# Moving the tiles of the weights' low parts to a pool that begins 128 bytes behind a whole row

## The chip, the cores and the metric

The kernel runs on 1 core of one Trainium2 chip. The metric is the device time of one execution in microseconds (us): the median of three timed runs. One further execution was recorded by the hardware profiler, and the rows below come from it.

## The reference

Two model blocks run one after the other on `x` of shape (1, 512, 1024), in float32. The first block has two layers. Each layer is a gated feed-forward network, a mixer with three branches (a Fourier mix, a dilated window attention, a differential attention) and another gated feed-forward network:

```
x = x + 0.5 * swiglu(rmsnorm(x, g_ffn1[l]), w_ffn1_gate[l], w_ffn1_up[l], w_ffn1_down[l])
u = rmsnorm(x, g_mix[l]);  p = u @ w_in[l]
merged = gates[0] * (fourier(p) @ w_br_a) + gates[1] * (dilated(p) @ w_br_b) + gates[2] * (diff(p) @ w_br_c)
x = x + merged @ w_out[l]
x = x + 0.5 * swiglu(rmsnorm(x, g_ffn2[l]), w_ffn2_gate[l], w_ffn2_up[l], w_ffn2_down[l])
```

The second block has one layer of stick-breaking attention beside a state-space mixer, and one layer of gated linear attention. Most of the arithmetic is products of the 512 tokens with weight matrices.

## The kernel before

**Products in three matmuls.** A float32 product is made from operands that are cut in two: `hi`, the value rounded to the type that TensorE takes at one column per cycle (float32r), and `lo`, what is left. `mm3` (L195 to L199) issues hi x hi (L197), hi x lo (L198) and lo x hi (L199) into the same bank of PSUM. `split` (L90 to L95) makes the two parts: ScalarE (ACT) copies the source into `hi` (L93), VectorE (DVE) subtracts `hi` from the source into `lo` (L94).

**Weights.** A chunk of weights is a block of up to 8 x 256 columns on 128 partitions. `weights` (L97) issues one DMA on SP's queue into a raw tile `wr`, then writes `wh` on ACT (L108) and `wl` on DVE (L109), in two halves of 128 columns. `weights7` (L113) does the same for a product that is made from seven smaller ones: `wh` and `wl` hold the parts of four of its operands, and tiles `sw` those of the other three. `setup` (L269) makes the first chunk, `odd` (L1496) one of 128 columns.

**How a chunk is used.** In `form_a`, `form_a2`, `form_a_late` and `form_a7` the weights are the stationary operand (loaded by a LDWEIGHTS, row PEld in the profile) and the tokens `xh`, `xl`, `g` or `sb` are the moving operand, 512 or 256 columns. In `form_b` it is the other way round: the tokens are loaded, and 256 columns of `wh` or `wl` move. In the profile a matmul's name is `b<-moving,stationary`, so `b<-xh,wl` at L199 loads a block of `wl` and moves `xh`.

**Order and waits.** The program is written in one order for each engine. The Tile framework puts in the waits, by the bytes that instructions read and write. TensorE (PE) works through the list; DMA, ACT and DVE prepare the next chunks while it does, two buffers for each of `wr`, `wh` and `wl`.

**Where the tiles lie.** Pools of tiles lie one behind the other in a partition of SBUF. A tile of 512 float32 takes 2,048 bytes; this is the row that the title speaks of. The pool `cp` has the eight tiles `x`, which begin 128 bytes behind a whole row, and constants: the identity `cc` begins 928 bytes behind a whole row (416 behind a multiple of 512), `ntri` 960 and `nones` 448 (both 448 behind a multiple of 512). The pool `wp` begins on byte 36,864, which is 18 whole rows, with `wr`, `wh` and `wl`, two buffers of 8,192 bytes each. The pool `sp` follows, with tiles of 2,048 bytes (`g`, `sw`, `s`, `xh`, `xl`) and four of 5,120 (`sb`). A block that TensorE loads is 128 columns, 512 bytes. So each of L197 to L199's operands begins at a multiple of 512 bytes. The pool `sm`, with tiny tiles of sums and scales, is last.

Of the kernel before, what the change touches and what calls it, by code (L numbers as in the profile page):

```python
# [9 lines left out]
F32 = mybir.dt.float32  # L10
F32R = mybir.dt.float32r
# [6 lines left out]
P = 128  # L18
S = 512
D = 1024  # L20
KD = D // P
# [29 lines left out]
class Kern:  # L51
    def __init__(self, ctx, tc, ins, out, dbg=None):
        self.tc, self.nc, self.ins, self.out, self.dbg = tc, tc.nc, ins, out, dbg
        self.cp = ctx.enter_context(tc.tile_pool(name="cp", bufs=1))
        self.wp = ctx.enter_context(tc.tile_pool(name="wp", bufs=2))
        self.sp = ctx.enter_context(tc.tile_pool(name="sp", bufs=2))
        self.sm = ctx.enter_context(tc.tile_pool(name="sm", bufs=8))
        self.ps = ctx.enter_context(tc.tile_pool(name="ps", bufs=8, space=PSUM))
        self.dp = ctx.enter_context(tc.tile_pool(name="dp", bufs=1, space=DRAM))
        self.n = 0  # L60

    def nm(self, s):
        self.n += 1
        return f"{s}{self.n}"
# [25 lines left out]
    def split(self, src, hi=None, lo=None):  # L90
# [3 lines left out]
        self.nc.vector.tensor_tensor(out=lo, in0=src, in1=hi.bitcast(F32), op=ALU.subtract)  # L94
        return hi, lo  # L95

    def weights(self, src, k0=0, nk=None):  # L97

        nc = self.nc
        src = src[:, k0:k0 + nk, :] if nk is not None else src  # L100
        _, nk, n = src.shape
        raw = self.wp.tile([P, nk, n], F32, tag="wr", name=self.nm("wr"), bufs=2)
        nc.sync.dma_start(raw, src)
        hi = self.wp.tile([P, nk, n], F32R, tag="wh", name=self.nm("wh"))
        lo = self.wp.tile([P, nk, n], F32R, tag="wl", name=self.nm("wl"))
        for j in range(0, n, P):
            js = slice(j, j + P)
            nc.scalar.activation(hi[:, :, js], raw[:, :, js], AF.Copy)  # L108
            nc.vector.tensor_tensor(out=lo[:, :, js], in0=raw[:, :, js], in1=hi.bitcast(F32)[:, :, js],  # L109
                                    op=ALU.subtract)  # L110
        return hi, lo

    def weights7(self, src):  # L113


        nc = self.nc
        raw = self.wp.tile([P, KD, 256], F32, tag="wr", name=self.nm("wr"), bufs=2)
        nc.sync.dma_start(raw, src)
        hi = self.wp.tile([P, KD, 256], F32R, tag="wh", name=self.nm("wh")).rearrange("p k n -> p (k n)")
        lo = self.wp.tile([P, KD, 256], F32R, tag="wl", name=self.nm("wl")).rearrange("p k n -> p (k n)")  # L120
        h = KD // 2
        v3 = lambda t: t.rearrange("p (k n) -> p k n", n=P)
        a = {(i, j): raw[:, j * h:(j + 1) * h, i * P:(i + 1) * P] for i in range(2) for j in range(2)}
        at = [v3(hi[:, i * S:(i + 1) * S]) for i in range(4)], [v3(lo[:, i * S:(i + 1) * S]) for i in range(4)]

        def parts(x, i=None):
            o = (at[0][i], at[1][i]) if i is not None else (v3(self.spare("sw", 6, F32R)), v3(self.spare("sw", 6, F32R)))
            return self.split(x, *o)

        both = v3(hi[:, 0:2 * S]), v3(lo[:, 0:2 * S])  # L130
        self.split(raw[:, :, 0:P], *both)
        a11, a12 = [(at[0][i], at[1][i]) for i in range(2)]
        a22 = parts(a[1, 1], 2)
        s1, s2 = v3(self.spare("s", 2)), v3(self.spare("s", 2))
        self.tt(s1, a[1, 0], a[1, 1], ALU.add)
        p1 = parts(s1, 3)
        self.tt(s2, s1, a[0, 0], ALU.subtract)
        p2 = parts(s2)
        self.tt(s1, a[0, 0], a[1, 0], ALU.subtract)
        p3 = parts(s1)  # L140
        self.tt(s2, a[0, 1], s2, ALU.subtract)
        p4 = parts(s2)
        return {1: a11, 2: a12, 3: p4, 4: a22, 5: p1, 6: p2, 7: p3}
# [125 lines left out]
    def setup(self):  # L269
        nc, ins = self.nc, self.ins  # L270
        self.x = [self.const([P, S], f"x{k}") for k in range(KD)]
        cols = self.const([P, NPAR], "par")
        nc.sync.dma_start(cols, ins["params"])
        warm = self.const([P, 1], "warm")
        nc.vector.memset(warm, 0.0)
        self.act(warm, warm, AF.Silu)

        raw, hi, lo = (self.wp.tile([P, KD, 256], dt, tag=t, name=self.nm(t), bufs=2)
                       for t, dt in (("wr", F32), ("wh", F32R), ("wl", F32R)))
        for k in range(KD):  # L280
            if k % 2 == 0:
                ks = slice(k, k + 2)
                nc.sync.dma_start(raw[:, ks, :], ins["w_ffn1_gate"][0][0][:, ks, :])
                self.split(raw[:, ks, :], hi[:, ks, :], lo[:, ks, :])
            nc.sync.dma_start(self.x[k], ins["x"][k])
        self.first = hi, lo
        self.par, at = {}, 0
        for name, n in PARAMS:
            self.par[name] = cols[:, at:at + n]
            at += n  # L290
        cc = self.const([P, NCONST], "cc")
        nc.sync.dma_start(cc, ins["c_mats"])
        self.ident, self.tri = cc[:, 0:P], cc[:, P:2 * P]
        self.ones = self.const([P, P], "ones")
        nc.vector.memset(self.ones, 1.0)
        one = self.const([P, 2], "one")
        nc.vector.memset(one[:, 0:1], -0.5)
        nc.vector.memset(one[:, 1:2], E32)
        self.mhalf, self.e32 = one[:, 0:1], one[:, 1:2]
        self.nones, self.ntri = self.const([P, P], "nones"), self.const([P, P], "ntri")  # L300
        nc.vector.memset(self.nones, -1.0)
        self.ts(self.ntri, self.tri, -1.0, ALU.mult)
        self.bglu = self.const([P, 4], "bglu")
        self.ts(self.bglu, self.par["s5_b_glu_2"], 0.5, ALU.mult)
        self.bh = self.const([P, 48], "bh")
        self.ts(self.bh, self.par["b_gate"], 0.5, ALU.mult)
# [1189 lines left out]
    def odd(self):  # L1496
# [5 lines left out]
        raw = self.wp.tile([P, KD, P], F32, tag="wr", name=self.nm("wr"), bufs=2)  # L1502
        gp.memset(raw, 0.0)
        nc.sync.dma_start(raw[:, :, 0:16], ins["odd_w_r"])
        w = (self.wp.tile([P, KD, P], F32R, tag="wh", name=self.nm("wh")),
             self.wp.tile([P, KD, P], F32R, tag="wl", name=self.nm("wl")))
        self.split(raw, *w)
        wgt = self.g()
        gp.memset(wgt, 0.0)
# [336 lines left out]
```

## Time and profile before

| | |
|---|---|
| median of three runs | 3041.65 us (3041.04 to 3041.98) |
| the profiled execution's own time | 3038.39 us |
| its span, first to last instruction | 3036.7 us |
| granted clock of TensorE, mean | 1.0 |
| PE busy | 3015.5 us |
| PEld busy | 2645.0 us |
| DVE busy | 2037.7 us |
| ACT busy | 1352.4 us |
| DMA | 311.14 MB, 102 GB/s mean |

The busy time of PE is the time in which at least one matmul was under way. Matmuls are pipelined: the next begins before the last has ended, so the duration of one is longer than the time that it costs. What a matmul costs in a full stream is the distance from its start to the start of the next, which is read from the timeline.

### The profile page before, as it was taken

To read this page: it belongs to the slowest core of one execution; us is meant where nothing else is said; L and a number is where in the kernel's file an instruction comes from. 1 tells how busy PE (TensorE), PEld (TensorE's weight loads), DVE (VectorE), ACT (ScalarE), POOL (GpSimd) and SP (SyncE) were. 2 spreads that over 40 slices of the span, in tenths; PEclk is the share of its full clock that TensorE was granted. 3 is DMA by queue.
4 is the path that set the end of the run, shared out by engine and by line. 5 is a ranking of instruction groups with operands and counts; after the bars stand their busy time and mean duration, and the time that the engine had idled before them with its cause. 6 is when DMAs were issued, how large, how long until landed. Compare 5 with 4: busy or idle time off the path is not lost.

```text
span 3036.7 us, 44149 instructions
## 1 busy us (share of the span) xinstructions
PE 3015.5 (99%) x17718; PEld 2645.0 (87%) x17718; DVE 2037.7 (67%) x3646; ACT 1352.4 (45%) x2380; POOL 177.8 (6%) x310
## 2 busy tenths in 40 slices
PE   9999999999999999999999999999999999999999
PEld 7898889889889988889988889888999898877887
DVE  7798745646567979878874565557788855554633
ACT  5343435544343435433433554444334456663532
POOL 1001000000000011001120000000000011110010
PEclk9999999999999999999999999999999999999999
DMA  4232333322222333223343432222232332312221
GB/s 153 105 103 105 118 108 115 111 78 98 92 90 98 114 121 121 98 98 110 107 140 108 122 108 91 75 97 91 104 112 89 124 131 100 108 53 84 95 70 56
DMA packets 73358, 311.14 MB, mean 102 GB/s; under 512 B 18836, under 2 KB 20564, under 8 KB 44608
## 3 DMA queue, kind: packets, MB, share of 16 engines
q1 hardware_dynamic: 59680, 282.39, 27.0%
q10 hardware_dynamic: 9296, 16.47, 1.9%
q0 software_dynamic: 4176, 9.46, 1.2%
q8 instruction: 139, 2.28, 0.3%
q14 instruction: 67, 0.55, 0.1%
HBM read 292.47 MB, written 12.66 MB: 100 GB/s over the span
## 4 chain that ended last, share of the span: by engine, by line
PE 94%; ACT 2%; issue 1%; DVE 1%; DMA 1%; POOL 0%; SPq 0%; POOLq 0%; ACTq 0%; DVEq 0%
PE b L197 29%; PE b L199 29%; PE b L198 29%; PE b L202 7%; PE b L266 2%; ACT g L250 1%; ACT L250 0%; ACT sb L250 0%; DMA g<-tb 0%; DVE wl L109 0%; POOL sb L1259 0%; POOL y L240 0%; DVE g L240 0%; DMA g<-s_kst 0%; DMA wr<-in_w_ffn_gate 0%
## 5 line engine op out<-in xcount | busy, mean ns | idle before, releaser
L197 PE MATMUL b<-xh,wh 128*128 128x512 f32 (+1 forms) x1880 | 692.6, 368 | 7.3 <-ACT xh L250 6.8
L198 PE MATMUL b<-xl,wh 128*128 128x512 f32 (+1 forms) x1880 | 682.4, 363 | 1.1 <-DVE xl L94 1.1
L199 PE MATMUL b<-xh,wl 128*128 128x512 f32 (+1 forms) x1880 | 682.8, 363 | 0.5 <-DVE wl L94 0.5
L108 ACT ACTIVATE wh<-wr 128x1024 fp32r<-128x1024 f32 (+2 forms) x396 | 383.2, 1005 | 537.2 <-PE b L198 350.3
L109 DVE TENSOR_TENSOR wl<-wr,wh 128x1024 fp32r<-128x1024 f32 (+2 forms) x396 | 453.2, 1162 | 137.0 <-ACT wh L108 135.4
L197 PE MATMUL b<-g,wh 128*128 128x512 f32 x1168 | 456.6, 391 | 0.5 <-ACT g L93 0.5
L199 PE MATMUL b<-g,wl 128*128 128x512 f32 x1168 | 454.8, 389 | 1.2 <-DVE wl L109 1.2
L198 PE MATMUL b<-g,wh 128*128 128x512 f32 x1168 | 454.8, 389 | 0.2 <-DVE g L94 0.2
L197 PEld LDWEIGHTS b<-xh,wh 128*128 128x128 f32 x1880 | 355.7, 189 | 62.4 <-ACT xh L250 6.8
L198 PEld LDWEIGHTS b<-xl,wh 128*128 128x128 f32 x1880 | 355.8, 189 | 57.3 <-issue 2.2
L199 PEld LDWEIGHTS b<-xh,wl 128*128 128x128 f32 x1880 | 355.2, 189 | 57.8 <-DVE wl L94 0.9
L240 DVE TENSOR_TENSOR g<-b,g 128x512 f32<-128x512 f32 (+2 forms) x265 | 184.2, 699 | 235.3 <-PE b L199 220.8
L199 PEld LDWEIGHTS b<-g,wl 128*128 128x128 f32 x1168 | 219.2, 188 | 47.9 <-DVE wl L109 2.0
L197 PEld LDWEIGHTS b<-g,wh 128*128 128x128 f32 x1168 | 219.3, 188 | 47.5 <-issue 2.0
L198 PEld LDWEIGHTS b<-g,wh 128*128 128x128 f32 x1168 | 219.3, 188 | 45.3 <-DVE g L94 0.5
L197 PE MATMUL b<-wh,xh 128*128 128x256 f32 x896 | 256.9, 287 | 0.0
L198 PE MATMUL b<-wl,xh 128*128 128x256 f32 x896 | 254.5, 284 | 1.0 <-DVE wl L109 1.0
L199 PE MATMUL b<-wh,xl 128*128 128x256 f32 x896 | 253.6, 283 | 0.0
L240 DVE TENSOR_TENSOR g<-g,g 128x512 f32<-128x512 f32 (+8 forms) x371 | 200.8, 570 | 66.7 <-ACT g L250 62.3
L240 DVE TENSOR_TENSOR g<-g,b 128x256 f32<-128x256 f32 (+1 forms) x484 | 176.9, 397 | 31.2 <-PE b L199 27.3
L93 ACT ACTIVATE sw<-s 128x512 fp32r<-128x512 f32 x180 | 111.8, 630 | 193.3 <-DVE s L240 159.2
L250 ACT ACTIVATE g<-g 128x512 f32<-128x512 f32 (+4 forms) x280 | 143.6, 528 | 96.5 <-DVE g L240 88.3
(242 smaller groups left out, 5117.2 us busy)
## 6 DMA issues: line engine op xcount, KB each, us to landing
wr<-in_w_ffn_up SPq DMA_DIRECT2D x44, 1024.0 KB, 4.8
wr<-in_w_ffn_gate SPq DMA_DIRECT2D x43, 1024.0 KB, 4.8
wr<-in_w_ffn_down SPq DMA_DIRECT2D x32, 1024.0 KB, 4.8
wr<-in_w_gate SPq DMA_DIRECT2D x24, 1024.0 KB, 4.8
wr<-in_w_in SPq DMA_DIRECT2D x20, 1024.0 KB, 4.8
wr<-in_even_w_in SPq DMA_DIRECT2D x20, 1024.0 KB, 5.1
wr<-in_w_ffn_down SPq DMA_DIRECT2D x16, 768.0 KB, 4.3
g<-tb ACTq DMA_DIRECT2D x48, 256.0 KB, 3.1
```

The source lines that it names most:

```text
L93: self.nc.scalar.activation(hi, src, AF.Copy)
L108: nc.scalar.activation(hi[:, :, js], raw[:, :, js], AF.Copy)
L109: nc.vector.tensor_tensor(out=lo[:, :, js], in0=raw[:, :, js], in1=hi.bitcast(F32)[:, :, js], op=ALU.subtract)
L197: t.matmul(out, l[0], r[0], start=start, stop=False)
L198: t.matmul(out, l[0], r[1], start=False, stop=False)
L199: t.matmul(out, l[1], r[0], start=False, stop=stop)
L202: self.nc.tensor.matmul(out, l, r, start=start, stop=stop)
L240: return (eng or self.nc.vector).tensor_tensor(out=out, in0=a, in1=b, op=op)
L250: self.nc.scalar.activation(out, a, f, **kw)
L266: self.nc.tensor.transpose(out, a, self.ident)
```

## The change

A new pool `lp` with two buffers of 8,192 bytes takes the tiles `wl`, and a pool `pp` ahead of it has one tile of 128 bytes that nothing uses. Each `wl` is now a view of a flat tile of 2,048 elements; its bytes inside the tile are in the same order as before. `wp` is shorter by 16,384 bytes, so that the tiles of `sp` lie eight rows lower, still on the same place in a row. `sp` ends on byte 204,800, which is 100 whole rows, and the two `wl` begin 128 bytes behind a whole row, at 204,928 and 213,120. No instruction is added or taken away, and the calls are in the same order.

```diff
         self.sp = ctx.enter_context(tc.tile_pool(name="sp", bufs=2))
+        self.pp = ctx.enter_context(tc.tile_pool(name="pp", bufs=1))
+        self.lp = ctx.enter_context(tc.tile_pool(name="lp", bufs=2))
         self.sm = ctx.enter_context(tc.tile_pool(name="sm", bufs=8))
...
+        self.pp.tile([P, 32], F32, name="pad")
...
+    def low(self, nk, n):
+
+        t = self.lp.tile([P, KD * 256], F32R, tag="wl", name=self.nm("wl"))
+        return t[:, 0:nk * n].rearrange("p (k n) -> p k n", n=n)
+
     def weights(self, src, k0=0, nk=None):
...
-        lo = self.wp.tile([P, nk, n], F32R, tag="wl", name=self.nm("wl"))
+        lo = self.low(nk, n)
...
-        lo = self.wp.tile([P, KD, 256], F32R, tag="wl", name=self.nm("wl")).rearrange("p k n -> p (k n)")
+        lo = self.low(KD, 256).rearrange("p k n -> p (k n)")
...
-        raw, hi, lo = (self.wp.tile([P, KD, 256], dt, tag=t, name=self.nm(t), bufs=2)
-                       for t, dt in (("wr", F32), ("wh", F32R), ("wl", F32R)))
+        raw, hi = (self.wp.tile([P, KD, 256], dt, tag=t, name=self.nm(t), bufs=2) for t, dt in (("wr", F32), ("wh", F32R)))
+        lo = self.low(KD, 256)
...
-             self.wp.tile([P, KD, P], F32R, tag="wl", name=self.nm("wl")))
+             self.low(KD, P))
```

## Rows read from the trace of the kernel before

**Rows 1.** The page: busy time of each engine, share of the span, instructions.
```profile
PE 3015.5 (99%) x17718; PEld 2645.0 (87%) x17718; DVE 2037.7 (67%) x3646; ACT 1352.4 (45%) x2380; POOL 177.8 (6%) x310
```

**Rows 2.** Waits of PE: for whom, us in total, times, longest.
```profile
PE b L197 <- ACT xh L250: 6.8, 1, 6.8
...
PE b L199 <- DVE wl L109: 1.2, 1, 1.2
...
PE b L198 <- DVE wl L109: 1.0, 1, 1.0
...
PE b L199 <- DVE wl L94: 0.5, 1, 0.5
```

**Rows 3.** PE's groups by line and shape: count | busy us, mean ns | idle before.
```profile
L199 PE MATMUL b<-xh,wl 128*128 128x512 f32 x1400 | 547.0, 391 | 0.5 <-DVE wl L94 0.5
...
L199 PE MATMUL b<-g,wl 128*128 128x512 f32 x1168 | 454.8, 389 | 1.2 <-DVE wl L109 1.2
...
L198 PE MATMUL b<-wl,xh 128*128 128x256 f32 x896 | 254.5, 284 | 1.0 <-DVE wl L109 1.0
...
L199 PE MATMUL b<-xh,wl 128*128 128x256 f32 x480 | 135.8, 283 | 0.0
...
L199 PE MATMUL b<-sb,wl 128*128 128x256 f32 x480 | 135.8, 283 | 0.0
```

**Rows 4.** PE's timeline, 512 columns, behind other work: start us, duration, instruction.
```profile
442.86 0.39 PE L198 MATMUL b<-xl,wh 128*128 128x512 f32 x1
443.09 0.40 PE L199 MATMUL b<-xh,wl 128*128 128x512 f32 x1
...
445.17 0.39 PE L199 MATMUL b<-xh,wl 128*128 128x512 f32 x1
...
447.66 0.39 PE L198 MATMUL b<-xl,wh 128*128 128x512 f32 x1
```

**Rows 5.** PE's timeline, 256 columns, weights moving.
```profile
476.89 0.28 PE L197 MATMUL b<-wh,xh 128*128 128x256 f32 x1
477.01 0.28 PE L198 MATMUL b<-wl,xh 128*128 128x256 f32 x1
...
478.81 0.28 PE L198 MATMUL b<-wl,xh 128*128 128x256 f32 x1
```

**Rows 6.** Busy time in two stretches: PE, PEld, DVE, ACT, POOL, clock, DMA.
```profile
444.90:452.00 7.10, 7.10 (x44) 6.25 (x44) 1.93 (x8) 2.49 (x7) 0.00 (x0) 1.00 0.54 181
477.00:482.00 5.00, 5.00 (x45) 5.00 (x43) 4.12 (x9) 2.77 (x7) 0.00 (x0) 1.00 0.77 228
```

**Rows 7.** PE's timeline, plain float32 matmuls with constants or tokens loaded.
```profile
2484.41 0.59 PE L202 MATMUL b<-g,nones 128*128 128x256 f32 x2
2484.84 0.59 PE L202 MATMUL b<-sb,ntri 128*128 128x256 f32 x2
2485.27 0.39 PE L202 MATMUL b<-sb,nones 128*128 128x128 f32 x2
2485.49 0.28 PE L202 MATMUL b<-sb,ntri 128*128 128x128 f32 x1
...
2498.09 2.32 PE L202 MATMUL b<-sb,g 128*128 128x512 f32 x8
2500.17 0.36 PE L197 MATMUL b<-wh,xh 128*128 128x256 f32 x1
```

**Rows 8.** Groups of DVE and ACT by line and shape.
```profile
L109 DVE TENSOR_TENSOR wl<-wr,wh 128x1024 fp32r<-128x1024 f32 x328 | 395.1, 1221 | 117.0 <-ACT wh L108 115.4
...
L240 DVE TENSOR_TENSOR g<-g,g 128x512 f32<-128x512 f32 x219 | 145.3, 687 | 64.0 <-ACT g L250 61.5
...
L240 DVE TENSOR_TENSOR x<-x,g 128x512 f32<-128x512 f32 x96 | 65.9, 688 | 1.7
...
L250 ACT ACTIVATE g<-g,y 128x512 f32<-128x512 f32 x80 | 57.1, 715 | 81.1 <-DVE y L244 81.1
...
L250 ACT ACTIVATE xh<-x,par 128x512 fp32r<-128x512 f32 x56 | 39.6, 715 | 55.3 <-DVE x L247 24.4 <-DVE x L240 23.8 <-PE b L199 7.0
```

## The prediction

> **What bounds the kernel now.** I read the page's first part, then PE's waits, then PE's groups by shape, then its timeline. The first shows that PE is the bound: it is busy for 3015.5 us of 3036.7, where DVE has 2037.7 and ACT 1352.4 [rows 1]. The second shows that it hardly ever waits for the tiles that are moved: 1.2, 1.0 and 0.5 us, one wait each [rows 2]. So a low part that is ready sooner, or a DVE that writes it faster, is worth 2.7 us at most, 0.09%. What can move the time is the distance from one matmul's start to the next.
>
> That distance is in the timeline. In a settled stream of 512 columns, 11 matmuls go from 445.17 to 447.66: 226.4 ns each [rows 4]. In a stream of 256 columns, 16 go from 476.89 to 478.81: 120.0 ns each [rows 5]. The granted clock is 1.00 in both stretches [rows 6], the 2.4 GHz level, at which 512 columns are 213.3 ns and 256 are 106.7. So each matmul of `mm3` costs 13 ns more than its columns, whether it has 512 or 256.
>
> Plain float32 matmuls go over their operand twice (two records for each), and there the extra is almost gone: two records of 256 columns go from 2484.84 to 2485.27, 215 ns each, and two of 128 from 2485.27 to 2485.49, 110 ns each [rows 7]. 215 and 110 against 226.4 and 120.0 is what a matmul of `mm3` could at best lose: 11.4 and 10.0 ns.
>
> **The change, part by part.** No instruction is added, removed or reordered, and no transfer. Three things are different: where `wl` lies, where the tiles of `sp` lie, and how `wl` is described to the framework.
>
> *DVE and ACT.* 328 pieces of 1,024 elements at L109 take 1221 ns [rows 8]; they now write at another place of a row. The nearest rows for such a place are the tiles `x`, which begin 128 bytes behind a row already: adding into `x` takes DVE 688 ns, and the same shape among `g`, on whole rows, 687; ACT reads `x` in 715 ns and `g` in 715 [rows 8]. So nothing changes there. If a piece were longer by 10 ns, 328 of them are 3.3 us, beside PE, which waits 2.7 us for them in the whole run [rows 2]; and if that cover were gone the 3.3 us would be the cost. I take 0.
>
> *`sp` eight rows lower.* Each tile keeps its place in a row. I take 0; the settled 226.4 and 120.0 hold over tiles of many rows, so that which rows meet seems to cost nothing.
>
> *TensorE.* A low part is read by PE in two ways. As the stationary operand of L199: 1400 + 1168 = 2568 matmuls of 512 columns and 480 + 480 = 960 of 256. As the moving operand of L198: 896 of 256 [rows 3]. That is 2568 long and 1856 short matmuls. Up to now the two operands that PE reads at a time in `mm3` both begin at a multiple of 512 bytes; in these 4424 they will be 128 bytes apart in that sense. The trace has no matmul of `mm3` with another place, so I bound the cost from both sides by the nearest rows.
>
> Below: all of the extra goes, 2568 x 11.4 ns + 1856 x 10.0 ns = 29.3 + 18.6 = 47.9 us. Above: the stream behaves as it does behind other work. From 443.09 to 445.17 nine matmuls take 231.1 ns each, before it settles at 226.4 [rows 4]; 2568 x 4.7 ns = 12.1 us, or 36.2 us if all three matmuls of each product (7704) stay unsettled. For 256 columns I take no loss.
>
> Which end is near? Three things speak for nothing at all. First, the float32 matmuls with a constant loaded (448 behind a multiple of 512) take 0.86 us for 1,024 columns from 2484.41 to 2485.27, 0.84 ns a column; those with tokens loaded, both operands on a multiple, take 2.08 us for 2 x (512 + 384 + 256 + 128) = 2,560 columns from 2498.09, 0.81 ns [rows 7]. Meeting at the same place is no dearer there. Second, from 477 to 482 DVE was busy for 4.12 us of 5.00, ACT for 2.77 and DMA at 0.77 [rows 6], and the 120.0 ns inside it [rows 5] did not move; if places in SBUF collided, theirs should show too. Third, the extra is the same 13 ns for 512 and 256 columns, though the loads fill 6.25 of 7.10 us of the one stretch and all of the other [rows 6]. That looks like a price of each matmul. Against it stands the unsettled stretch [rows 4]: a fixed price would not be 18 ns in one stretch and 13 in the next, with the same tiles and lines, where only the phase between loading and moving can differ. So the two streams do touch each other, and a shift might matter. I take 0 and keep both ends.
>
> The Trainium skill gives two rules here that pull apart. TensorE: Matmul & The Clock Gate, section Back-to-back issue gap, has N / 2.4 + 2.5 ns for a warm stream, 215.8 ns for 512 columns; the 226.4 of the trace is longer, so by that page 10.6 ns of each long matmul are something that could go, 27 us over the 2568. SBUF — State Buffer, section Who interferes with whom, gives PE two independent read ports and says that PE never waits on anyone; by it the place of a tile costs nothing and the sum is 0. The trace agrees with neither entirely: the gap is longer than the first has it, and the unsettled stretch is not what the second would lead one to expect.
>
> *The description.* `wl` is now a view of a flat tile. Its bytes are in the same order, so that waits by bytes are the same. If they were not, PE would wait for a chunk's second half where it now needs the first alone, up to 1.22 us of DVE [rows 8] in each of the few places where the chunk is late; ten of them would be 12 us.
>
> The sum is 0 against the profiled execution's 3038.39 us (span 3036.7 and 1.7 around it). The median of the timed runs lies 3.3 us above that execution, and I forecast the median: 3041.5 us. About 0.2%, 6 us, is what a measurement of this kernel can tell from no change; the three runs lie within 0.9 us.
>
> **The rivals.**
>
> *Faster: the extra is a collision of the load with the moving stream.* If operands that begin at the same place within 512 bytes read the same part of the memory at once, the 128 bytes take the low part out of the other's way. For it: the phase matters [rows 4]; the extra vanishes where columns move at half the rate [rows 7]. Against it: the three points above. It gives up to 47.9 us, 2993.6 us; half of it 3017. It decides as soon as 1.4 ns of each of the 4424 go, 6 us.
>
> *Slower: the stream doesn't settle.* Today load and move fall into a fixed phase after some ten matmuls, and keep it [rows 4]. With one operand in three shifted, the phase may be kicked in every product, and the long matmuls cost 231.1 ns. It gives 12.1 us for the low parts alone, 3054 us, and 36.2 us for all, 3078 us. It decides from 2.4 ns of each of the 2568. For it: the length of the unsettled stretch. Against it: tokens and weights of very different tiles follow each other now without a kick.
>
> *Slower: coarser waits,* ten late chunks, 12 us, 3054 us. Against it: the bytes are the same.
>
> *The change doesn't do what it says* is not a rival of its own: `wl` does lie 128 bytes off; that this means nothing is my forecast.
>
> **How the numbers follow.** No change 0.53; faster by the collision 0.27; slower by the stream 0.16, by waits 0.04. So faster 0.27, same 0.53, slower 0.20. The likeliest case's own range is 3036 to 3047. The range of 8 in 10 must take in most of the faster case, whose end is 2994, and of the slower, of which I leave out the part above 3056: 2994 to 3056.
>
> **What would show it.** Right: in the new timeline 512 columns still take 226 to 227 ns from start to start, also where the next load is `wl`, and 256 take 120; `wl<-wr,wh` stays at 1221 ns; PE's waits for DVE at L198 and L199 stay near 2.7 us. Collision: the matmul before or at L199 starts its successor after some 216 ns, or L198 with `wl` moving after 110. Unsettled: some 231 all along. Waits: new rows of PE L199 for `wl`. I am wrong if the distance differs between matmuls that touch `wl` and those that don't.

## The result, and the profile after

The changed kernel takes 3058.65 us (median of six runs, 3057.7 to 3060.81), the one before 3041.65 (six runs, 3038.45 to 3044.84): the ratio is 1.0059, 95% interval 1.0048 to 1.0069. It is 17.0 us slower. The forecast was 3041.5 with a range up to 3056, so the time lies 2.65 us outside it, on the side to which 0.20 was given. The profiled execution took 3058.77 us, its span is 3057.0, 20.3 us more than before, at a granted clock of 0.999, the 2.4 GHz level.

What stands between the 17.0 and the 20.3 is the clock, as far as the records show. In the profile before, the granted clock, once risen at the start, is 1.00 until the matmuls end; in the profile after it falls to 0.50, the 1.2 GHz level, at 2752.4 us, behind waits of PE of 0.54 and 0.64 us for `xh` and `xl`, and some matmuls of 512 columns take 0.42 or 0.43 us from start to start. Executions with a mean clock of 1.000 took 3057.7 to 3058.54 us after and, in the later comparisons, 3038.5 to 3039.25 us before; so at the same clock the change costs some 19 us.

The page after, busy time of each engine (to be read beside [rows 1]; `mm3` is now L205 to L207, `weights` writes `wl` at L117):

```profile
PE 3037.2 (99%) x17718; PEld 2645.9 (87%) x17718; DVE 2037.9 (67%) x3646; ACT 1352.0 (44%) x2380; POOL 177.5 (6%) x310
```

PE's busy time is up by 21.7 us; DVE's and ACT's have not moved. So nothing is late, the matmuls themselves take longer. The waits of PE (us in total, times, longest; beside [rows 2]) and the group of DVE that writes the low parts (beside [rows 8]) agree with that:

```profile
PE b L205 <- ACT xh L258: 7.1, 1, 7.1
...
PE b L206 <- DVE wl L117: 0.6, 1, 0.6
...
PE b L207 <- DVE wl L97: 0.5, 1, 0.5
PE b L207 <- DVE wl L117: 0.4, 1, 0.4
```

```profile
L117 DVE TENSOR_TENSOR wl<-wr,wh 128x1024 fp32r<-128x1024 f32 x328 | 395.0, 1221 | 119.0 <-ACT wh L116 106.1 <-PE b L210 11.3
```

PE waits 1.5 us for low parts in the whole run, and a piece of `wl` takes the 1221 ns that it took before. PE's groups with `wl` by shape (count, busy us, mean ns, idle before; beside [rows 3]) show where to look:

```profile
L207 PE MATMUL b<-xh,wl 128*128 128x512 f32 x1400 | 556.2, 397 | 0.5 <-DVE wl L97 0.5
...
L207 PE MATMUL b<-g,wl 128*128 128x512 f32 x1168 | 464.0, 397 | 0.4 <-DVE wl L117 0.4
...
L206 PE MATMUL b<-wl,xh 128*128 128x256 f32 x896 | 253.0, 282 | 0.6 <-DVE wl L117 0.6
...
L207 PE MATMUL b<-xh,wl 128*128 128x256 f32 x480 | 135.4, 282 | 0.0
```

The long ones are 6 and 8 ns longer than in [rows 3], the short ones 1 or 2 ns shorter: the two widths move in opposite directions. Such a duration overlaps with the next matmul, so the cost is read from the timeline (start, duration). First 512 columns, behind other work as in [rows 4], then 256 columns with weights moving, as in [rows 5]:

```profile
449.16 0.39 PE L206 MATMUL b<-xl,wh 128*128 128x512 f32 x1
449.39 0.40 PE L207 MATMUL b<-xh,wl 128*128 128x512 f32 x1
449.62 0.39 PE L205 MATMUL b<-xh,wh 128*128 128x512 f32 x1
449.85 0.40 PE L206 MATMUL b<-xl,wh 128*128 128x512 f32 x1
...
451.93 0.40 PE L206 MATMUL b<-xl,wh 128*128 128x512 f32 x1
```

```profile
480.82 0.28 PE L206 MATMUL b<-wl,xh 128*128 128x256 f32 x1
...
481.88 0.28 PE L206 MATMUL b<-wl,xh 128*128 128x256 f32 x1
```

From 449.16 to 451.93 there are 12 long matmuls, 230.8 ns each, where the settled stream before had 226.4 [rows 4]; from 480.82 to 481.88 there are nine short ones, 117.8 ns each, where it was 120.0 [rows 5]. That neither dies out is shown by the same count over the whole of both traces, by the place of a matmul in its product of three (mean start-to-start distance to the next matmul of the same kind, distances over 300 ns left out; the last two columns are the number of products and what they make in us):

| ns | before | after | products | us |
|---|---|---|---|---|
| 512 columns: hi x hi to hi x lo | 227.4 | 227.5 | | |
| 512 columns: hi x lo to lo x hi | 227.2 | 232.4 | | |
| 512 columns: lo x hi to next product | 227.4 | 233.9 | | |
| 512 columns, sum of three | 681.9 | 693.8 | 2568 | +30.6 |
| 256 columns, weights move, sum of three | 362.7 | 356.1 | 896 | -5.9 |
| 256 columns, tokens move, sum of three | 360.0 | 358.1 | 1776 | -3.4 |

The last column adds up to 21.3 us, against 20.3 in the span. At 512 columns the distance that leads to the matmul with the low part loaded, and the one behind it, are dearer; the one that touches no low part is unchanged. This is the sign that the prediction named as the one that would prove it wrong.

### The profile page after: what moved, and what is told of

Read it like the earlier page. It is cut to its first block, busy times and chain, and to the rows that moved or that the text cites. A ratio compares the mean times of both kernels' runs of the same rounds, so it can differ in the third digit from the quotient of the medians.

```text
span 3057.0 us, 44149 instructions
## 1 busy us (share of the span) xinstructions
PE 3037.2 (99%) x17718; PEld 2645.9 (87%) x17718; DVE 2037.9 (67%) x3646; ACT 1352.0 (44%) x2380; POOL 177.5 (6%) x310
## 4 chain that ended last, share of the span: by engine, by line
PE 95%; ACT 2%; issue 1%; DVE 1%; DMA 0%; POOL 0%; SPq 0%; POOLq 0%; ACTq 0%; DVEq 0%
PE b L206 29%; PE b L207 29%; PE b L205 28%; PE b L210 7%; PE b L274 2%; ACT g L258 1%; ACT L258 0%; ACT sb L258 0%; POOL sb L1267 0%; DVE wl L117 0%; POOL y L248 0%; DMA g<-s_kst 0%; DMA g<-tb 0%; DMA wr<-in_w_ffn_gate 0%; DVE g L248 0%
## 5 line engine op out<-in xcount | busy, mean ns | idle before, releaser
L205 PE MATMUL b<-xh,wh 128*128 128x512 f32 (+1 forms) x1880 | 692.2, 368 | 7.6 <-ACT xh L258 7.1
L207 PE MATMUL b<-xh,wl 128*128 128x512 f32 (+1 forms) x1880 | 691.6, 368 | 0.5 <-DVE wl L97 0.5
L206 PE MATMUL b<-xl,wh 128*128 128x512 f32 (+1 forms) x1880 | 690.6, 367 | 1.0 <-DVE xl L97 1.0
L117 DVE TENSOR_TENSOR wl<-wr,wh 128x1024 fp32r<-128x1024 f32 (+2 forms) x396 | 453.0, 1161 | 139.4 <-ACT wh L116 126.5
L207 PE MATMUL b<-g,wl 128*128 128x512 f32 x1168 | 464.0, 397 | 0.4 <-DVE wl L117 0.4
L205 PE MATMUL b<-g,wh 128*128 128x512 f32 x1168 | 457.1, 391 | 0.3 <-ACT g L96 0.3
L205 PEld LDWEIGHTS b<-xh,wh 128*128 128x128 f32 x1880 | 359.2, 191 | 68.2 <-ACT xh L258 7.1
L207 PEld LDWEIGHTS b<-xh,wl 128*128 128x128 f32 x1880 | 354.2, 188 | 57.8 <-DVE wl L97 0.9
L205 PEld LDWEIGHTS b<-g,wh 128*128 128x128 f32 x1168 | 224.2, 192 | 52.8 <-issue 2.0
L207 PEld LDWEIGHTS b<-g,wl 128*128 128x128 f32 x1168 | 219.4, 188 | 47.4 <-DVE wl L117 1.5
L205 PE MATMUL b<-wh,xh 128*128 128x256 f32 x896 | 254.2, 284 | 0.0
L207 PE MATMUL b<-wh,xl 128*128 128x256 f32 x896 | 250.7, 280 | 0.0
```

Source lines behind the costliest of these rows:

```text
L205: t.matmul(out, l[0], r[0], start=start, stop=False)
L206: t.matmul(out, l[0], r[1], start=False, stop=False)
L207: t.matmul(out, l[1], r[0], start=False, stop=stop)
```

## The experiments

The theories, by the letters that the expectations use (those of the later runs are explained in their expectations). **K** (kick; the prediction's slower rival): it is the turn from one place to the other within a product that costs. **P**: the place itself costs, for each pair of a loaded and a moving block, turn or no turn. **W**: it is not the 128 bytes but the new pool, the flat view or the waits. After the first runs P was made sharper: **D**, only the distance from the moving to the loaded block counts, modulo 256 bytes; against **S**, a block off the row is dear whatever the other's place.

### The pool without the 128 bytes, and with 256

```diff
-        self.pp.tile([P, 32], F32, name="pad")
```

> The changed kernel without its 128 bytes: the pool and the flat view stay, but the low parts begin on a whole row again. K and P: the time of the kernel before, 3041.65 within 4 us. W: the time of the changed kernel, 3058.65.

Measured: 3041.3 us, ratio 1.0001 (0.9992 to 1.001). Pool, view and `sp` eight rows lower cost nothing, so W falls, and with it the prediction's rival of coarser waits. All of it comes from 128 bytes.

```diff
-        self.pp.tile([P, 32], F32, name="pad")
+        self.pp.tile([P, 64], F32, name="pad")
```

> The changed kernel with 256 bytes in place of 128. D: the time of the kernel before, 3041 within 4 us, and 226.7 ns again before and after a load of a low part. If it is the shift as such that costs (the low parts' pool off a whole row): 3050 or more.

Measured: 3041.95 us, ratio 1.0003 (0.9994 to 1.0012). At 256 bytes nothing happens either; the three sums of the table are 682.0, 362.7 and 360.0 ns. Being off the row is not the cause by itself.

### Both weights' parts 128 bytes behind

`wh` goes into the pool `lp` too, so that `wh` and `wl` have one place; the tokens stay on the row, and so do the tiles `sw`.

```diff
-        hi = self.wp.tile([P, nk, n], F32R, tag="wh", name=self.nm("wh"))
+        hi = self.lp.tile([P, nk, n], F32R, tag="wh", name=self.nm("wh"))
...
```

> High and low parts of the weights both begin 128 bytes behind a whole row, so that their distance to the tokens is the same in all three matmuls. K: no alternation among the weights, so the time of the kernel before, 3041 within 5 us. P: all three matmuls of a product pay, some 7 ns on 7704 long ones, 3090 us or more. W: as the changed kernel, 3058.

Measured: 3071.42 us, ratio 1.0103 (1.0089 to 1.0117), 30 us above before. Now there is no turn between places in a product of 512 columns, and all three distances are 232.5 ns. K falls: a constant 128 bytes costs in every matmul, about as much as a low part costs the two distances beside it. P's direction is right and its size too large: the bare lists (below) lose 5.7 to 6.7 ns in each long matmul, the kernel, whose stream is not settled everywhere, 5.2. The sums of three are 697.5 for 681.9 ns at 512 columns (+40.1 us over 2568), and the short ones give back 2.5 + 4.4 us, which P did not have.

### Bare matmuls at many places

Lists of 36 matmuls of the same pair, or of 72 with three pairs in turn, with nothing else going on (DVE, ACT, POOL and DMA are at 0.00 from 17 to 290 us of both runs, the granted clock at 1.00); the loaded block lies so many bytes behind a row, the moving one on the row, unless the name says otherwise. These kernels leave the whole computation out. In outline:

```
for w in PLACES:                            # by_zero, by_sixteen, ... loaded block
    run([(w, (move, 0))], 36, cols, ...)    # 512 or 256 columns
run([("zero", (shifted, 64))], ...)         # the moving block behind: "ahead", "far"
run([(z, m0), (z, m0), (o, m0)], ...)       # "low": every third load 128 behind
```

> This kernel leaves the whole computation out: it copies x to the output and runs bare float32r matmuls of 512 and then 256 columns in a row, with no waits, from tiles whose place in a row is chosen. Runs of one pattern each: the loaded block 0, 16, 32, 64, 96, 128, 192, 256, 384, 448 and 512 bytes behind a whole row with the moving operand on one; then moving 128 behind; then patterns of three like mm3's, with the low block, the high block, the low tokens, or both weights shifted. Theory K (kick): a constant distance between the two operands costs the same wherever it is, 226.7 ns for 512 columns and 120 for 256 in every run of one pattern, and only the run that alternates 0, 0, 128 costs more, 227, 232 and 234 ns in turn, as in the changed kernel. Theory P (place): the distance itself decides, so that single runs differ by several ns: 226.7 at 0 and 512, and about 233 at 128. Theory W (waits or order of the flat view): nothing here differs from 226.7 and 120, the pattern 0, 0, 128 included, for this kernel has no waits.

The list "low", whose every third load lies 128 bytes behind, in the timeline of that run (start, duration; x2 are two matmuls in one row).

```profile
141.36 0.40 PE L47 MATMUL long_low<-moving,by_onetwentyeight 128*128 128x512 f32 x1
141.59 0.62 PE L47 MATMUL long_low<-moving,by_zero 128*128 128x512 f32 x2
142.05 0.40 PE L47 MATMUL long_low<-moving,by_onetwentyeight 128*128 128x512 f32 x1
```

A product takes 0.69 us; over the last 30 distances the mean is 231.1 ns, one of 227, one of 232 or 233 and one of 234, in turn. This is the changed kernel's pattern, without DVE, ACT or DMA, so W falls here too. Where the moving block of one pair in three is 128 behind instead, only one of the three distances is dearer: 225.7, 226.6 and 234.4 ns. A list with all loads 128 behind is at 232.4, which K has at 226.7; one with the moving block 128 behind as well is at 226.65, as on the row: so it is the distance between the two that counts.

> Leaves the whole computation out, as the first kernel of bare matmuls did. It loads a block from each multiple of 16 bytes up to 240 behind a whole row beside a moving operand on one, 512 columns and then 256; then it puts the moving operand 64 and 192 bytes behind instead; then 128 columns, and plain float32 matmuls at 0, 64 and 128. Theory D (distance modulo 256): the distance from the moving operand to the loaded block, taken modulo 256 bytes, decides. The lowest long distance is 226.7 ns, at 0 and near it, and nothing goes below; short ones have one low place near 64, some 113 ns; moving 192 behind gives what loading 64 behind gave (113), and moving 64 behind what loading 192 behind gave (117.8). Theory S (shifted tile): any tile off the multiples pays or gains by its own place, so that moving 64 behind gives 113 too. Plain float32: 215 to 216 at all three places by both.

The second run takes every multiple of 16 bytes. A list is 36 matmuls; its time is from its start to that of the next row:

```profile
17.42 8.32 PE L50 MATMUL long_one<-moving,by_zero 128*128 128x512 f32 x36
25.58 8.33 PE L50 MATMUL long_one<-moving,by_sixteen 128*128 128x512 f32 x36
33.75 8.55 PE L50 MATMUL long_one<-moving,by_thirtytwo 128*128 128x512 f32 x36
42.14 8.56 PE L50 MATMUL long_one<-moving,by_fortyeight 128*128 128x512 f32 x36
...
84.10 8.56 PE L50 MATMUL long_one<-moving,by_onetwoeight 128*128 128x512 f32 x36
92.50 8.57 PE L50 MATMUL long_one<-moving,by_onefourfour 128*128 128x512 f32 x36
...
150.79 8.42 PE L50 MATMUL long_ahead<-shifted,by_zero 128*128 128x512 f32 x36
159.05 8.55 PE L50 MATMUL long_far<-shifted,by_zero 128*128 128x512 f32 x36
167.44 5.91 PE L50 MATMUL short_warm<-moving,by_zero 128*128 128x256 f32 x48
173.18 4.48 PE L50 MATMUL short_one<-moving,by_zero 128*128 128x256 f32 x36
177.50 4.42 PE L50 MATMUL short_one<-moving,by_sixteen 128*128 128x256 f32 x36
...
190.26 4.26 PE L50 MATMUL short_one<-moving,by_sixtyfour 128*128 128x256 f32 x36
194.36 4.44 PE L50 MATMUL short_one<-moving,by_eighty 128*128 128x256 f32 x36
...
281.95 7.07 PE L62 MATMUL plain_sixtyfour<-plain,pload 128*128 128x256 f32 x32
288.86 7.07 PE L62 MATMUL plain_onetwoeight<-plain,pload 128*128 128x256 f32 x32
```

Long lists: 8.16 us on the row (226.7 ns each), 8.39 at 32 and 8.40 at 128 (233.3). Short lists: 4.32 on the row (120.0), 4.10 at 64 (113.9 with the way in, 113.35 settled). The settled values by distance (mean of the last 20 of each list, ns):

| bytes | 0 | 16 | 32 | 64 | 96 | 128 | 160 | 192 | 224 | 240 |
|---|---|---|---|---|---|---|---|---|---|---|
| 512 columns | 226.7 | 226.7 | 233.3 | 233.3 | 234.5 | 233.4 | 233.4 | 228.9 | 233.4 | 226.7 |
| 256 columns | 120.0 | 118.2 | 118.4 | 113.4 | 118.7 | 118.7 | 120.1 | 117.8 | 116.7 | 120.0 |

The moving block 64 behind ("ahead") gives the 228.9 of 192, and 192 behind ("far") the 233.35 of 64; with 256 columns they give 117.75 and 113.3. Distances of 256 and 512 bytes were as 0 (226.7 and 120.0) in the run before. That is D, and S falls. One pair of lists in the run before does not fit the modulo: 384 bytes took 231.95 and 120.0 ns where 128 took 232.4 and 118.65. 128 columns take 111.65 ns, and each of the two records of a plain float32 matmul of 256 columns takes 215.8, at each of the places tried.

### The change in two halves

The low parts get a place by what they are used for: those that are loaded for 512 columns, or those of the sevens (the products that are made from seven smaller ones, in `form_a7`) and of `form_b`. A tile is 256 bytes longer, and the view begins 0 or 32 elements into it.

```diff
+LONG, SHORT = 32, 0        # low_long; 0, 32 in low_short
-    def low(self, nk, n):
+    def low(self, nk, n, at=None):
...
-        lo = self.low(KD, 256).rearrange("p k n -> p (k n)")
+        lo = self.low(KD, 256, SHORT).rearrange("p k n -> p (k n)")
...
-                w = self.weights(w_in[c])
+                w = self.weights(w_in[c], at=SHORT)
```

> The change alone for the weights whose blocks are loaded for 512 columns: their low parts lie 128 bytes behind a row, the low parts that serve matmuls of 256 columns lie on a row. Theory D (the distance of the loaded from the moving block, modulo 256 bytes, sets the pace of each pair): 2568 products by 13.4 ns (two of the three distances at 233.35 for 226.65 in the bare lists) make 34.4 us, so 3075 (3071 to 3079), above the changed kernel, whose short matmuls gave some 14 us back. Rival K2 (the loss needs both kinds shifted, because it comes when the stream passes from one to the other): 3041 to 3059.

> The other half of the change alone: the low parts that serve matmuls of 256 columns (the sevens' loaded blocks of the tiles wl, and the weights that move in form_b) lie 128 bytes behind a row, those for 512 columns on a row. Theory D with the changed kernel's own distances (weights that move 320.9 to 314.6 ns for three, the sevens a little below 120): 14 us less than before, 3027 (3023 to 3033). Theory D with the bare lists (short_low 119.10 for 120.0, 1856 products of three): 5 us less, 3036. Rival K2: 3041, no gain without the other half.

Measured: low_long 3068.98 us, ratio 1.0094 (1.0081 to 1.0108), so +27.74; low_short 3030.99, ratio 0.9971 (0.996 to 0.9982), so -10.25. Together +17.5, from 27.74 - 10.25; the whole change is +17.0, or some 19 at the same clock. So K2, by which low_short gains nothing and low_long stays at or below 3059, falls: each half does its part without the other. The pages of the two, low_long first:

```profile
PE 3046.2 (99%) x17718; PEld 2655.2 (87%) x17718; DVE 2039.3 (66%) x3646; ACT 1352.2 (44%) x2380; POOL 177.5 (6%) x310
```

```profile
PE 3007.7 (99%) x17718; PEld 2636.9 (87%) x17718; DVE 2038.1 (67%) x3646; ACT 1352.4 (45%) x2380; POOL 176.8 (6%) x310
```

The sums of three are those of the table, each half its own: low_long 693.8, 362.7, 360.0; low_short 682.0, 356.1, 358.1. low_long fell 2 us short of its range: 13.4 ns a product had been taken, the difference of two settled streams; but the kernel before, whose stream is not settled everywhere, took 681.9 ns for three and not 680, so that it lost 11.9. low_short lies between its two estimates, 14 us from the changed kernel's own distances and 5 us from the bare lists, and inside the range of the first.

### Distances that are better than before

If D is right, there are better places for 256 columns than the row. short_shifted starts from the kernel before: the sevens' loaded blocks (`wh`, `wl`, `sw`) lie 64 bytes behind the row, the weights that move in `form_b` 192 behind (so that the load is 64 ahead of them, modulo 256), and whatever serves 512 columns stays on it. seven_shifted has the first of the two alone.

```diff
+SEVEN, FORM_B = 16, 48     # elements of 4 bytes; 16, 0 in seven_shifted
...
-        hi = self.wp.tile([P, nk, n], F32R, tag="wh", name=self.nm("wh"))
-        lo = self.wp.tile([P, nk, n], F32R, tag="wl", name=self.nm("wl"))
+        hi, lo = self.part("wh", nk, n, at), self.part("wl", nk, n, at)
```

> From the kernel before, with the output complete: where short matmuls (256 columns) run, the loaded block is put 64 bytes ahead of the moving operand modulo 256: weights of the seven products 64 bytes behind a multiple of 256, the tiles sw too, and weights that move 192 behind; long matmuls keep the distance 0. Theory D: 7700 short matmuls at 113.35 instead of 120 ns are 51 us less, 2990 us, less whatever DVE then can't keep up with (it is busy for 4.1 to 4.8 us of 5 in such stretches), so 2990 to 3015. Theory S: the weights that move lose what the sevens gain, 3005 to 3030.

> The same with the weights of the seven products and the tiles sw alone; weights that move stay on multiples of 256. D: 5040 x 6.65 ns = 33.5 us less, 3008 us, or up to 3020 if DVE holds it up; the matmuls with weights moving stay at 120.

Measured: short_shifted 3016.13 us, ratio 0.9919 (0.9905 to 0.9933); seven_shifted 3029.77, ratio 0.9959 (0.9947 to 0.9972). Both are faster than before, and both miss D's ranges: the sevens came down to 117.9 ns (sum of three 353.7), not to the 113.35 of the bare list. The 3016.13 alone would lie in S's range, but S has the weights that move lose, and they gain: the second place brings another 13.6 us, and the sum of three of `form_b` goes from 362.7 to 350.1 ns. The next run put bare matmuls into the kernel's own order.

> Bare matmuls of 256 columns in the kernel's own order (high part with high, high with low, low with high; the blocks stepping through their tiles as the sevens and form_b do, accumulated, two halves of a bank); it leaves the whole computation out, so its total time says nothing. Theory D alone: the sevens' list settles at 113.35 ns where the loaded blocks lie 64 bytes behind the moving ones, and form_b's at 113.35 where the weights that move lie 192 bytes behind, as in the scan; then what kept the kernel at 117.8 is the other engines' traffic. Rival T (the order matters too: each block is loaded while the matmul ahead of it still moves, so two distances count for every pair): 117 to 118 at 64 here too, and one of the single steps (loaded blocks that step, moving blocks that step, accumulation, the two halves) takes 113.35 to 117 or 118 by itself. Which place is best for each list is read off the 16 places and the six mixed pairs.

Settled means of that run, ns, worked out from its trace:

```
sevens' order, 16 places:  0: 120.0   64: 113.3   192: 113.3   all others: 116.7 to 120.0
form_b's order, 16 places: 0: 120.0  112: 113.3   192: 113.3   all others: 116.7 to 120.0
sevens' order, high parts at 64 and low parts at 192: 113.3 ; high 192, low 64: 113.3
one fixed pair at 64, and with one thing added each (accumulation, two halves of a bank,
  low load in turn, low move in turn, loads that step, moves that step): 117.8 in all seven
```

Neither theory had this. T falls, since the full order runs at 113.3. The seven lists at 117.8 say less than they seem to: they follow each other at one distance, and each may have kept the pace in which the list ahead of it ran. But D alone is not the whole either: the fixed pair at 64 took 113.35 in the scan and 117.8 here, where the list ahead of it and the tiles' own addresses (by multiples of 256 bytes) are others. At the same distance there are two settled paces.

That the pace is carried on from what ran ahead can be read in the changed kernel's own trace. Four of the sevens load from `wh` and `wl`, three from `sw`, which lies on the row as before. Before, the sum of three is 360.0 ns in all of the three with `sw`, and in place_zero too. After, it is 356.8 and 357.0 ns in the two that follow directly behind products with a shifted `wl`, and 360.0 again in the one that follows another product with `sw`. So some 1.5 of the 3.4 us of the sevens in the table were gained where the distance is 0 (480 products by 3.1 ns).

The last two runs tried whether another place, or two, bring the kernel into the quicker one.

```diff
-SEVEN, FORM_B = 16, 48
+SEVEN, FORM_B = 48, 48                     # all_192
+SEVEN, SEVEN_LOW, FORM_B = 16, 48, 48      # high_64_low_192
...
```

The tiles `sw` move along; in high_64_low_192 their low parts are tiles of their own, `sx`.

> As short_shifted, with the sevens' loaded blocks 192 bytes behind a row instead of 64. The bare list in the kernel's order settled at 113.33 at 64 and at 192, but other bare lists with the same distance at 117.8, so there are two paces. Theory H (which of the two a list falls into is set by how it is entered, not by the place): the kernel has long stretches in which its entry is the same at both places, 117.8 again, 3016 (3012 to 3020). Rival B (192 is a better place than 64 for the sevens): about 5400 matmuls by up to 4.4 ns, down to 2992.

> As short_shifted, with the sevens' high parts 64 and their low parts 192 bytes behind a row. The bare list with these two places came out at 113.33 although the list ahead of it ran at 119. Theory H (the entry decides): 117.8 as with 64 alone, 3016 (3012 to 3020). Rival B (two places lead every list into the quicker pace): 113.33 in the sevens, about 5400 matmuls by 4.4 ns, 2992 (2988 to 2998).

Measured: all_192 3018.24 us, ratio 0.9924 (0.9907 to 0.994), the 117.9 ns of before in the sevens; high_64_low_192 2997.55, ratio 0.9855 (0.984 to 0.987). Theory H expected 3016 of both and is right on the first only; rival B is wrong on the first and right on the second. That the whole kernel reaches 113.3 also takes out the traffic of the other engines, which D alone had named in the expectation of the bare order, as what held it at 117.8. The sevens in the timelines, short_shifted first, then high_64_low_192:

```profile
71.93 0.28 PE L205 MATMUL b<-sb,wl 128*128 128x256 f32 x1
...
75.81 0.28 PE L205 MATMUL b<-xh,sw 128*128 128x256 f32 x1
```

```profile
71.86 0.28 PE L211 MATMUL b<-sb,wl 128*128 128x256 f32 x1
...
75.60 0.28 PE L211 MATMUL b<-xh,wl 128*128 128x256 f32 x1
```

33 matmuls lie between the two rows of each: 3.88 us are 117.6 ns each, 3.74 us are 113.3. The last kernel beats both of this case: by 43.9 us the one before, by some 61 the changed one, with the same instructions at other places. `form_b` stays at a mixture of 113 to 118 in it (sum of three 349.9). The sums of three of the sevens are 353.7 in all_192 and 341.2 in high_64_low_192. What decides between the two paces at one distance, and why two places lead into the quicker one, is not shown by these runs.

## Why the prediction was wrong

**What held.** PE is the bound and only the distance between starts moves the time. DVE and ACT write the low parts in the same 1221 ns; `sp` eight rows lower and the flat view cost nothing (place_zero 1.0001). PE's waits for low parts went from 2.7 to 1.5 us. The 2568 long products that it counted are the ones that became dearer. Of the short ones more moved than the 1856 that touch `wl`, as the products with `sw` show.

**The step that failed** is the one in which the cost for TensorE was chosen: "I take 0 and keep both ends". What was put at 0 came to +30.6 us for the long and -9.3 us for the short products in the profiled execution, because the pace depends on the distance between the loaded and the moving block. The rows of the three points for nothing were read rightly, and none of them spoke on the question. The float32 matmuls cost about the same at different places [rows 7], but the scan shows that plain float32 does so at each of the three places tried (215.85, 215.80, 215.85 ns), while float32r doesn't: the row came from a stream that lacks the effect. The other engines' traffic doesn't move the 120 ns [rows 6], but the effect is between PE's own load and its own moving stream: the bare lists have it with every other engine idle. And the same 13 ns for 512 and for 256 columns was no fixed price of a matmul: by the distance, one goes from 13.3 to 20 and the other from 13.3 down to 6.7 (233.3 - 213.3; 113.35 - 106.7). In the trace of before every operand of `mm3` began on a multiple of 512 bytes, so none of its rows could show a dependence on the place. The unsettled stretch [rows 4], which the prediction counted against its choice, was the one hint in that trace: bare lists begin as unevenly when the distance has just changed (229, 232 and 231 ns, then 226 to 227, at 512 bytes).

The rule on the side of the choice, in the Trainium skill's SBUF — State Buffer, section Who interferes with whom, is that PE's two read ports are independent and that PE never waits on anyone. The bare lists do not bear it out for these two streams: 226.7 or 233.3 ns by the distance between them, with nothing else going on.

**The bounds.** Below, 47.9 us by a load that no longer meets the moving stream: the sign is right for 256 columns (9.3 us, where 18.6 were allowed for fewer products) and wrong for 512, which were already on one of the cheapest of the 16 distances. The 215.8 ns from the formula of the Trainium skill (TensorE: Matmul & The Clock Gate, section Back-to-back issue gap; that section calls it the gap of an isolated matmul, where the prediction has it for a stream) was reached by no list of 512 columns, of which the quickest took 226.65. Above, 12.1 us for the low parts alone, which took one dearer distance in a product at 4.7 ns; two became dearer, by 5.2 and 6.5, so that in all 11.9 ns of each product count where 4.7 had been taken. "For 256 columns I take no loss" was right, and the gain that came instead was in the faster rival alone: no case had the one width lose while the other gains. That the time came within 2.65 us of the range is therefore luck: the long half alone takes 3068.98 us (low_long), and the short half, which no slower case had, gave part of it back.

**The rivals.** The slower one named the place (the long matmuls of L205 to L207, some 231 ns all along) and the direction, but its cause fell: not a phase that is kicked when the place changes, since a constant 128 bytes costs in every matmul (both_shifted) and 256 bytes in none (low_256). Its 3054 for the low parts alone was 4.6 us short. Its other end, 3078 with all three matmuls dearer, was left out of the range above 3056. Coarser waits fell with place_zero.

## What to carry to other kernels

Where PE is the bound in back-to-back float32r matmuls, try the distance of loaded and moving operand (address modulo 256 bytes) in bare lists before tiles are moved, and then in the kernel, for the sevens had 113.35 ns in the one and 117.9 in the other: here 512 columns want 0 or 16 on either side, and 256 columns want 64 or 192, in the sevens with another place for the low parts than for the high ones. Read start-to-start distances by the place in the product, over the whole trace; a change of 5 ns does not show in the waits, and the durations overlap. And a row speaks on an effect only if it could have shown it: where all operands of the trace have one place, it says nothing of another, however many matmuls it has.

## What was not expected of the hardware

- The pace of float32r matmuls depends on the distance of the two operands modulo 256 bytes, for 512 columns between 226.65 and 234.5 ns, for 256 between 113.3 and 120.1, in opposite directions from 0; not for 128 columns (111.65) nor plain float32 (215.8), at the places tried.
- With 512 columns, a load off the distance costs in two of the three distances of a product, its own and the one ahead of it (227.5, 232.4, 233.9 ns); a moving block off the distance costs in one (225.7, 226.6, 234.4 ns in bare lists).
- At one distance, 64 bytes, lists of one fixed pair with 256 columns settled at 113.35 ns in one run and at 117.8 in another, and each kept its pace to the end of the list. Products at distance 0 behind quicker ones ran at 356.8 ns for three instead of 360.0.
